# A fp32 convolution block with MLP on one core: seven output jobs as a 512- and a 256-column product a tile, with another evacuation

## The chip, the cores and the metric

The kernel runs on one core of one Trainium2 chip. The metric is the device time of one execution in microseconds (us). Three executions of the kernel before took 1066.16, 1066.22 and 1066.40 us; the median is 1066.22 us.

## The reference

```python
cond = jax.nn.silu(c)
mod = cond @ mod_w + mod_b
sh1, sc1, g1, sh2, sc2, g2 = jnp.split(mod, 6, axis=-1)
h = _rms_norm(x, norm1_g) * (1.0 + sc1) + sh1
y = _conv_mixer(h, conv_w_in, conv_b_in, ...)     # ends with u @ w_out + b_out
x = x + (1.0 + g1) * y
h = _rms_norm(x, norm2_g) * (1.0 + sc2) + sh2
u = jnp.square(jax.nn.relu(h @ mlp_w1))
x = x + (1.0 + g2) * (u @ mlp_w2)
```

There are 256 tokens and 2048 features; the MLP is 8192 wide. All is fp32. The part in question is `u @ w_out + b_out`, the gate `1 + g1`, the residual sum, and what the second norm and its shift `sh2` need from them.

## The kernel before

**Products.** Each fp32 operand is split in two fp32r halves, hi (the rounded value) and lo (the rest). A product is hi·hi + hi·lo + lo·hi. For weights `split_w` makes hi on ScalarE (L236) and lo on VectorE or GpSimd (L240), in two instructions a tile, each for 8 of the 16 blocks k of 128 input features. For activations `split_act` makes hi (L251, ScalarE) and lo (L254, VectorE), and they lie side by side as 512 columns.

**The output stage.** It lies from about 298 to 381 us. Job ("out", i), i = 0 to 7, makes 256 of the 2048 output features in two tiles c = 0, 1 of 128 features by 256 tokens. GpSimd makes lo for jobs 1 to 5, VectorE for jobs 6 and 7. Job 0 has a loop of its own (`mm_pair`). Jobs 1 to 7 call `mm(..., merged=True)`: for each k three products of 256 columns (L264 to L266) into one 256-column sum, both tiles in one PSUM tile `acc` of 512 columns, of which there are two. `mm` without `merged` makes two products for each k: L268, hi weights by the 512 columns, and L269, lo weights by the first 256, into the second half of a sum of 512 columns.

**Behind each job.** ScalarE applies the gate and a bias for each tile (L1419, in place in PSUM), VectorE adds 512 columns of x (L1420), ScalarE squares (L1422), GpSimd adds the squares up (L1427), ScalarE scales x by `1 + sc2` (L1431, into a tile `two` in SBUF), and L251 and L254 split that into `xa[i]`, the input of the first MLP jobs.

**Condition columns.** Beside the output jobs the 16 columns of `sh2` are made, each from 1 MB of `mod_w`: loaded by SyncE's queue into a `raw` buffer and multiplied with the condition on VectorE. Where the condition lies in PSUM (copied by L1441) that takes two instructions (L665), elsewhere one with two SBUF operands of 2048 columns (L669). The sum of the shift is copied by L1453 into `shz`, and `shift_row` (L600) multiplies it with the weights of ("up", 0) into a PSUM tile `row`.

**Behind job 7.** TensorE does a column sum of the squares (L695, ones by `sqacc`), the first 14 k of tile 0 of job ("up", 0, 0) with `xa[0]` to `xa[6]`, the column sum of job 7's squares (L695), L600, and then the products with `xa[7]`, the k 14 and 15.

**What orders the work.** The kernel is built by a scheduler that places each instruction by its data and its place in the code; `urgent()` puts a piece ahead, `tc.issue_after(x)` puts it behind x, and `after[job]` lists the columns that are made beside a job. `state["next_hi"]` is the weight split behind which job 6's L1419 goes. The instructions of one engine run strictly in the order that results.

Of the kernel before, what the change touches and what calls it, by code (L numbers as in the profile page):

```python
# [9 lines left out]
F32 = mybir.dt.float32  # L10
F32R = mybir.dt.float32r
AF = mybir.ActivationFunctionType
ALU = mybir.AluOpType
PSUM = bass.MemoryType.PSUM

P = 128
T = 256
# [18 lines left out]
SH1, SC1, G1, SH2, SC2, G2 = range(6)  # L36
# [51 lines left out]
def conv_block(ctx: ExitStack, tc: tile.TileContext, x, vec, dwq, c_row, mod_r, mod_t, mod_c, w_first, w_in, w_out, w1, w2, out):  # L88
    nc = tc.nc
# [49 lines left out]
    state = {"used": 0}  # L139
# [12 lines left out]
    def urgent():  # L152
        return tc.high_priority(offset=URGENT)
# [95 lines left out]
    def split_act(dst, src, on_act=True):  # L249
        if on_act:  # L250
            state["hi_end"] = nc.scalar.activation(dst[:, :, 0:T], src, AF.Copy).ins  # L251
        else:
            nc.vector.tensor_copy(dst[:, :, 0:T], src)
        state["lo_end"] = nc.vector.tensor_tensor(dst[:, :, T : 2 * T], src, dst[:, :, 0:T].bitcast(F32), op=ALU.subtract).ins  # L254

    def mm(p, c, key, acts_of, ks=range(KT), merged=False):
        halves = parts[key]
        for k in ks:
            hi, lo = halves[k // HALF]
            m = acts_of[k // 2][:, k % 2, :]  # L260
            if merged:
                out_p, begin, end = p[:, c, 0:T], k == 0, k == KT - 1
                w = hi[:, k % HALF, :]
                nc.tensor.matmul(out_p, w, m[:, 0:T], start=begin, stop=False)  # L264
                nc.tensor.matmul(out_p, w, m[:, T : 2 * T], start=False, stop=False)  # L265
                state["mm_end"] = nc.tensor.matmul(out_p, lo[:, k % HALF, :], m[:, 0:T], start=False, stop=end)  # L266
                continue
            nc.tensor.matmul(p[:, c, :], hi[:, k % HALF, :], m, start=(k == 0), stop=(k == KT - 1))  # L268
            state["mm_end"] = nc.tensor.matmul(  # L269
                p[:, c, T : 2 * T], lo[:, k % HALF, :], m[:, 0:T], start=False, stop=(k == KT - 1),  # L270
                skip_group_check=True,
            )
# [25 lines left out]
    def mm_tokens(sums, job, acts_of, last):  # L298
        steps = [(k, r) for k in range(HALF) for r in sums]
        if last:  # L300
            steps = [(k, r) for r in sums for k in range(HALF)]
        for k, (t, cs, p) in steps:
            hi, lo = [w[:, 4 * (k % 2) : 4 * (k % 2) + 4, :].rearrange("p k n -> p (k n)")[:, cs]
                      for w in parts[job + (k // 4,)][k // 2 % 2]]
            at = HALF * (job[2] % 2) + k
            m = acts_of[at // 2][:, at % 2, :]
            shared = job[0] == "down" and job[1] in EIGHT
            begin, end = at == 0 or shared and job[2] == 1 and t == 1 and at == HALF, at == KT - 1
            p_hi, p_lo = [m[:, n : n + P] for n in (t * P, T + t * P)]
            nc.tensor.matmul(p, p_hi, hi, start=begin, stop=False, skip_group_check=shared)  # L310
            nc.tensor.matmul(p, p_hi, lo, start=False, stop=False, skip_group_check=shared)  # L311
            nc.tensor.matmul(p, p_lo, hi, start=False, stop=end, skip_group_check=shared)  # L312

    def run_tasks():
        state["job"] += 1
        with tc.issue_after(state["w_lo"]), tc.issue_after(state["w_hi"]):
            for task in tasks.pop(state["job"], []):
                task()
# [371 lines left out]
    def mcol(which, k):  # L690
        return modc[:, which * KT + k : which * KT + k + 1]
# [21 lines left out]
    def ps_two():  # L713
        return ps.tile([P, 2, T], F32, name="acc", bufs=2)

    def two():
        return tmp.tile([P, 2, T], F32, name="two", bufs=6)

    def pair_of(tiles, k2):
        if tiles is xs:  # L720
            return xs[:, 2 * k2 : 2 * k2 + 2, :]
        return tiles[k2 // 2][:, 2 * (k2 % 2) : 2 * (k2 % 2) + 2, :]
# [51 lines left out]
    after = {}  # L774
# [34 lines left out]
    def splits(job):  # L809
        if job[0] == "eight":  # L810
            with urgent():
                split_eight(*job[1:])
            return
        if job[0] == "seven":
            with urgent():
                split_seven(*job[1:])
            return
        for c in range(2):
            if job + (c,) in parts_early:
                continue  # L820
            on_pool = job[0] == "in" or job in POOLED
            with urgent(), behind(c):
                split_w(job + (c,), nc.gpsimd if on_pool else nc.vector)
            if c == 0:
                state["next_hi"] = state["w_hi"]
                if job[0] in ("up", "down"):
                    with urgent():
                        run_tasks()

    def evac(p, cs=slice(0, 2), out=None):  # L830
        t1 = two()[:, cs, :]
# [347 lines left out]
    for n, job in enumerate(jobs):  # L1179
# [49 lines left out]
                    top_up()  # L1229
            continue  # L1230
        if kind == "out" and i > 0:
            p = ps_two()
        elif not by_tokens(job):
            p = ps.tile([P, 2, 2 * T], F32, name="mm", bufs=2)
        if by_tokens(job) and (i % 2 == 0 or kind == "down" and job[1] in EIGHT and i < 4):
# [2 lines left out]
        if job == ("up", 0, 0):  # L1238
            mm(p, 0, job + (0,), xa, range(SIDE))
            for at in range(2 * UNSCALED):  # L1240
                shift_row(at, shown.pop(("up", 0, at // 2, at % 2)))
            fold_shift()
            mm(p, 0, job + (0,), xa, range(SIDE, KT))
            mm(p, 1, job + (1,), xa)
        elif job == ("out", 0):
            for k2 in range(HALF):
                with tc.issue_after(state["row_end"].ins) if k2 == 1 else ExitStack():
                    mm_pair(p, job, k2)
                if k2 == 0:
                    with tc.issue_after(state["mm_end"].ins):  # L1250
                        mod_chunk(*last_row[0][1:], last_row[1])
        elif job in K_OUTER:
            for k2 in range(HALF):
                for c in range(2):
                    mm(p, c, job + (c,), xa if plain else hl, range(2 * k2, 2 * k2 + 2))
        elif kind == "in":
            rows = [key for key in after[job] if key[0] != "col"] if i < KT - 1 else []
            for c in range(2) if i < KT - 1 else (1, 0):
                for ks in (range(HALF), range(HALF, KT)):
                    with tc.issue_after(state.pop("rows_end")) if "rows_end" in state else ExitStack():  # L1260
                        mm(p, c, job + (c,), hl, ks, i == KT - 1)
            if not CONV_AT.get(n):
                with tc.issue_after(state["mm_end"].ins):
                    mods(rows)
                state["rows_end"] = state["row_end"].ins
        elif by_tokens(job):
            mm_tokens(sums[kind, i // 2], job, u2 if kind == "down" else hl, n == len(jobs) - 1)
        else:
            for c in range(2):
                mm(p, c, job + (c,), hl, merged=kind == "out")  # L1270
        with tc.issue_after(state["mm_end"].ins) if kind == "in" else ExitStack():
            mod_finish()
        if n == KT - 3:
# [136 lines left out]
        if kind == "out":  # L1410
            if i == 0:
                xs = take(("x", 0))
            t2 = p[:, :, 0:T]
            xp = pair_of(xs, i)
            with urgent():
                for c in range(2):
                    k = 2 * i + c
                    with tc.issue_after(state["next_hi"]) if i == HALF - 2 else ExitStack():
                        nc.scalar.activation(t2[:, c, :], t2[:, c, :], AF.Identity, scale=mcol(G1, k), bias=gb[:, k : k + 1])  # L1419
                nc.vector.tensor_tensor(xp, t2, xp, op=ALU.add)  # L1420
            ss = two()
            nc.scalar.activation(ss, xp, AF.Square)  # L1422
            if i == 0:
                nc.gpsimd.tensor_tensor(sqacc, ss[:, 0, :], ss[:, 1, :], op=ALU.add)
            elif i < HALF - 1:
                for c in range(2):
                    nc.gpsimd.tensor_tensor(sqacc, sqacc, ss[:, c, :], op=ALU.add)  # L1427
            a = two()
            for c in range(2):
                k = 2 * i + c  # L1430
                nc.scalar.activation(  # L1431
                    a[:, c, :], pair_of(xs, i)[:, c, :], AF.Copy, scale=amps[SC2][:, k : k + 1]
                )
            xa[i] = mp.tile([P, 2, 2 * T], F32R, name="u2", bufs=HALF)
            split_act(xa[i], a)
            if i == IN_PSUM[0]:
                state["cond"] = []
                for h in range(2):
# [3 lines left out]
                    state["cond"].append(half)  # L1442
            if i == IN_PSUM[-1] + 1:
                del state["cond"]
            mods(after[job])
            if i == HALF - 2:
                table(AF.Abs_reciprocal_sqrt, ss[:, 0, 0:1])
            if i == HALF - 1:
# [147 lines left out]
```

## Time and profile before

| | |
|---|---|
| median of three executions | 1066.22 us |
| profiled execution | 1066.46 us |
| its span | 1064.7 us |
| TensorE busy | 1046.3 us (98%) |
| VectorE busy | 911.7 us (86%) |
| ScalarE busy | 601.5 us (56%) |
| GpSimd busy | 222.3 us (21%) |
| DMA, mean over the span | 311 GB/s |

The span is cut out of the profiled execution; 1.8 us lie around it. Busy time is the union of an engine's instructions. In a timeline "x4" is a run of four like instructions with the time of all; "[0.58 <-DVE u L254]" is idle time of the engine ahead of the row and what ended it. L numbers are lines of the kernel before, except where the text says of the change. Matmul records overlap: the pace is the distance from start to start. PE is TensorE, DVE VectorE, ACT ScalarE, POOL GpSimd, SP SyncE.

### The profile page before, as it was taken

The page shows a single profiled execution, that of the slowest core. Times are in us where ns is not written, and L with a number is a line of the kernel's source. Part 1 is how long each engine was busy: PE and PEld are TensorE (multiplying, and loading weights), DVE is VectorE, ACT ScalarE, POOL GpSimd, SP SyncE. Part 2 cuts the span into 40 slices and gives each one's busy share as a digit, 9 for nine tenths or more (in the row PEclk, how much of TensorE's full clock was granted, in tenths as well). Part 3 has the DMA queues.
Part 4 walks back from the last instruction along what each step waited for, and adds up shares of the span by engine and source line. Part 5 has one row for each costly group of instructions (what it writes and reads, how often), then busy time and mean ns, then how long its engine had stood idle before and what let it go on. Part 6 is the DMA issues. An engine that isn't in the chain of part 4 may idle for free.

```text
span 1064.7 us, 15463 instructions
## 1 busy us (share of the span) xinstructions
PE 1046.3 (98%) x5776; PEld 865.1 (81%) x5776; DVE 911.7 (86%) x1191; ACT 601.5 (56%) x831; POOL 222.3 (21%) x153
## 2 busy tenths in 40 slices
PE   6999999999999999999999999999999999999998
PEld 3888886678699988888888888888888888888886
DVE  5777789998766889878799899899999899899996
ACT  4111298866775585344546565745566744656751
POOL 0000078989689272000000000000000000000001
PEclk8999999999999999999999999999999999999999
DMA  9999997996999976999996998693989796899853
GB/s 381 421 420 420 415 419 315 356 396 237 404 399 406 409 259 261 322 312 327 320 327 248 340 277 271 240 388 108 366 244 321 249 335 179 290 282 347 216 148 59
DMA packets 154333, 330.99 MB, mean 311 GB/s; under 512 B 88465, under 2 KB 114321, under 8 KB 119313
## 3 DMA queue, kind: packets, MB, share of 16 engines
q1 hardware_dynamic: 153248, 328.30, 85.1%
q0 software_dynamic: 864, 1.57, 1.1%
q8 instruction: 45, 0.74, 0.3%
q14 instruction: 30, 0.25, 0.1%
q10 hardware_dynamic: 146, 0.13, 0.0%
HBM read 313.71 MB, written 17.83 MB: 311 GB/s over the span
## 4 chain that ended last, share of the span: by engine, by line
PE 83%; DMA 10%; DVE 5%; ACT 1%; issue 1%; SPq 0%; DVEq 0%; ACTq 0%
PE mm L311 12%; PE mm L312 12%; PE mm L310 12%; DMA raw<-mod_c 9%; PE mm L268 6%; PE mm L269 3%; PE acc L265 3%; PE acc L264 3%; PE acc L266 3%; PE mm L1094 2%; PE row L576 2%; PE acc L485 2%; PE acc L486 2%; PE acc L484 1%; DVE raw L669 1%; DVE lo L240 1%
## 5 line engine op out<-in xcount | busy, mean ns | idle before, releaser
L236 ACT ACTIVATE hi<-raw 128x1024 fp32r<-128x1024 f32 x374 | 383.9, 1055 | 257.7 <-PE mm L312 127.6
L240 DVE TENSOR_TENSOR lo<-raw,hi 128x1024 fp32r<-128x1024 f32 x313 | 371.0, 1217 | 52.4 <-ACT hi L236 51.8
L240 POOL TENSOR_TENSOR lo<-raw,hi 128x1024 fp32r<-128x1024 f32 x61 | 155.8, 2581 | 30.1 <-ACT hi L236 29.8
L669 DVE SCALAR_TENSOR_TENSOR raw<-raw,cond 128x2048 f32<-128x2048 f32 x50 | 117.7, 2356 | 25.2 <-DMA raw<-mod_c 25.2
L460 POOL DMA_DIRECT2D out<-two x6 | 5.4, 902 | 639.2 <-DVE two L458 629.8
L311 PE MATMUL mm<-lo,u 128*128 128x512 f32 x320 | 124.5, 389 | 0.0
L312 PE MATMUL mm<-hi,u 128*128 128x512 f32 x320 | 124.0, 389 | 0.0
L310 PE MATMUL mm<-hi,u 128*128 128x512 f32 x320 | 123.8, 389 | 0.0
L310 PE MATMUL mm<-hi,hl 128*128 128x512 f32 x288 | 112.1, 389 | 0.0
L312 PE MATMUL mm<-hi,hl 128*128 128x512 f32 x288 | 112.1, 389 | 0.0
L311 PE MATMUL mm<-lo,hl 128*128 128x512 f32 x288 | 112.1, 389 | 0.0
L973 DVE SCALAR_TENSOR_TENSOR acc<-u,v,acc 128x256 f32<-128x256 f32 x230 | 91.5, 482 | 0.0
L268 PE MATMUL mm<-hl,hi 128*128 128x512 f32 x256 | 91.1, 399 | 0.0
L269 PE MATMUL mm<-hl,lo 128*128 128x256 f32 x256 | 71.7, 280 | 0.0
L310 PEld LDWEIGHTS mm<-hi,u 128*128 128x128 f32 x320 | 60.1, 188 | 12.6
L312 PEld LDWEIGHTS mm<-hi,u 128*128 128x128 f32 x320 | 60.1, 188 | 12.4
L311 PEld LDWEIGHTS mm<-lo,u 128*128 128x128 f32 x320 | 60.1, 188 | 12.4
L877 PE MATMUL mm<-two,first 128*128 128x256 f32 x240 | 56.7, 391 | 8.5 <-ACT two L935 8.5
L264 PE MATMUL acc<-hl,hi 128*128 128x256 f32 x224 | 63.4, 283 | 0.0
L265 PE MATMUL acc<-hl,hi 128*128 128x256 f32 x224 | 63.4, 283 | 0.0
L266 PE MATMUL acc<-hl,lo 128*128 128x256 f32 x224 | 63.4, 283 | 0.0
L310 PEld LDWEIGHTS mm<-hi,hl 128*128 128x128 f32 x288 | 54.1, 188 | 11.3
(383 smaller groups left out, 2018.8 us busy)
## 6 DMA issues: line engine op xcount, KB each, us to landing
raw<-w SPq DMA_DIRECT2D x128, 1024.0 KB, 7.6
raw<-mod_c SPq DMA_DIRECT2D x64, 1024.0 KB, 11.5
raw<-mod_r SPq DMA_DIRECT2D x28, 1024.0 KB, 8.7
raw<-w_in SPq DMA_DIRECT2D x16, 1024.0 KB, 10.6
raw<-w_out SPq DMA_DIRECT2D x16, 1024.0 KB, 8.2
first<-w_first SPq DMA_DIRECT2D x15, 1024.0 KB, 19.8
u<-kept SPq DMA_DIRECT2D x24, 512.0 KB, 7.6
flat<-two SPq DMA_DIRECT2D x30, 256.0 KB, 7.8
```

What stands on the lines that cost most here:

```text
L236: state["w_hi"] = nc.scalar.activation(hi, w[:, ks, :], AF.Copy).ins
L240: end = by.tensor_tensor(lo, w[:, ks, :], hi.bitcast(F32), op=ALU.subtract)
L264: nc.tensor.matmul(out_p, w, m[:, 0:T], start=begin, stop=False)
L265: nc.tensor.matmul(out_p, w, m[:, T : 2 * T], start=False, stop=False)
L266: state["mm_end"] = nc.tensor.matmul(out_p, lo[:, k % HALF, :], m[:, 0:T], start=False, stop=end)
L268: nc.tensor.matmul(p[:, c, :], hi[:, k % HALF, :], m, start=(k == 0), stop=(k == KT - 1))
L269: state["mm_end"] = nc.tensor.matmul(p[:, c, T : 2 * T], lo[:, k % HALF, :], m[:, 0:T], start=False, stop=(k == KT - 1), skip_group_check= ...
L310: nc.tensor.matmul(p, p_hi, hi, start=begin, stop=False, skip_group_check=shared)
L311: nc.tensor.matmul(p, p_hi, lo, start=False, stop=False, skip_group_check=shared)
L312: nc.tensor.matmul(p, p_lo, hi, start=False, stop=end, skip_group_check=shared)
L669: end = nc.vector.scalar_tensor_tensor(w, w, 1.0, cb, op0=ALU.mult, op1=ALU.mult, accum_out=acc)
L973: end = nc.vector.scalar_tensor_tensor(out, s, w, acc, op0=ALU.mult, op1=ALU.add)
```

## The change

Jobs 1 to 7 no longer merge: each k is L268 and L269, into a 512-column sum of its own for each tile, so that the two `acc` buffers hold one tile each. The bias is added to x in advance on ScalarE (`add_bias`, L1421 of the change). A tile is evacuated by two VectorE instructions of 256 columns (L1445 of the change), x += gate · half; the second waits for the first. ScalarE's L1419 and VectorE's L1420 remain for job 0 alone. The scaled x goes to PSUM, into the tiles `small` and `row` in turn (L1463 of the change), and L251 and L254 read it there; job 7 has `row`. The columns of `after[job]` are split between the two tiles and put behind the evacuation of each. The copies of the condition (L1431 of the change) stand ahead of the evacuation, and `next_hi` is gone.

```diff
--- before.py
+++ after.py
@@ -821,11 +821,9 @@
             on_pool = job[0] == "in" or job in POOLED
             with urgent(), behind(c):
                 split_w(job + (c,), nc.gpsimd if on_pool else nc.vector)
-            if c == 0:
-                state["next_hi"] = state["w_hi"]
-                if job[0] in ("up", "down"):
-                    with urgent():
-                        run_tasks()
+            if c == 0 and job[0] in ("up", "down"):
+                with urgent():
+                    run_tasks()
 
     def evac(p, cs=slice(0, 2), out=None):
         t1 = two()[:, cs, :]
@@ -1229,7 +1227,7 @@
                     top_up()
             continue
         if kind == "out" and i > 0:
-            p = ps_two()
+            p = [ps_two().rearrange("p a t -> p (a t)")[:, None, :] for _ in range(2)]
         elif not by_tokens(job):
             p = ps.tile([P, 2, 2 * T], F32, name="mm", bufs=2)
         if by_tokens(job) and (i % 2 == 0 or kind == "down" and job[1] in EIGHT and i < 4):
@@ -1265,9 +1263,12 @@
                 state["rows_end"] = state["row_end"].ins
         elif by_tokens(job):
             mm_tokens(sums[kind, i // 2], job, u2 if kind == "down" else hl, n == len(jobs) - 1)
+        elif kind == "out":
+            for c in range(2):
+                mm(p[c], 0, job + (c,), hl)
         else:
             for c in range(2):
-                mm(p, c, job + (c,), hl, merged=kind == "out")
+                mm(p, c, job + (c,), hl)
         with tc.issue_after(state["mm_end"].ins) if kind == "in" else ExitStack():
             mod_finish()
         if n == KT - 3:
@@ -1410,29 +1411,18 @@
         if kind == "out":
             if i == 0:
                 xs = take(("x", 0))
-            t2 = p[:, :, 0:T]
             xp = pair_of(xs, i)
-            with urgent():
+
+            def add_bias(k2, after):
                 for c in range(2):
-                    k = 2 * i + c
-                    with tc.issue_after(state["next_hi"]) if i == HALF - 2 else ExitStack():
-                        nc.scalar.activation(t2[:, c, :], t2[:, c, :], AF.Identity, scale=mcol(G1, k), bias=gb[:, k : k + 1])
-                nc.vector.tensor_tensor(xp, t2, xp, op=ALU.add)
-            ss = two()
-            nc.scalar.activation(ss, xp, AF.Square)
+                    k = 2 * k2 + c
+                    s = pair_of(xs, k2)[:, c, :]
+                    with urgent(), tc.issue_after(after):
+                        nc.scalar.activation(s, s, AF.Identity, bias=gb[:, k : k + 1])
+
             if i == 0:
-                nc.gpsimd.tensor_tensor(sqacc, ss[:, 0, :], ss[:, 1, :], op=ALU.add)
-            elif i < HALF - 1:
-                for c in range(2):
-                    nc.gpsimd.tensor_tensor(sqacc, sqacc, ss[:, c, :], op=ALU.add)
-            a = two()
-            for c in range(2):
-                k = 2 * i + c
-                nc.scalar.activation(
-                    a[:, c, :], pair_of(xs, i)[:, c, :], AF.Copy, scale=amps[SC2][:, k : k + 1]
-                )
-            xa[i] = mp.tile([P, 2, 2 * T], F32R, name="u2", bufs=HALF)
-            split_act(xa[i], a)
+                for k2 in (1, 2):
+                    add_bias(k2, state["silu"])
             if i == IN_PSUM[0]:
                 state["cond"] = []
                 for h in range(2):
@@ -1442,7 +1432,40 @@
                     state["cond"].append(half)
             if i == IN_PSUM[-1] + 1:
                 del state["cond"]
-            mods(after[job])
+            cols = list(after[job])
+            with urgent():
+                if i == 0:
+                    t2 = p[:, :, 0:T]
+                    for c in range(2):
+                        nc.scalar.activation(t2[:, c, :], t2[:, c, :], AF.Identity, scale=mcol(G1, c), bias=gb[:, c : c + 1])
+                    nc.vector.tensor_tensor(xp, t2, xp, op=ALU.add)
+            for c in range(2) if i else ():
+                with urgent():
+                    for a in range(2):
+                        end = nc.vector.scalar_tensor_tensor(
+                            xp[:, c, :], p[c][:, 0, T * a : T * a + T], mcol(G1, 2 * i + c), xp[:, c, :],
+                            op0=ALU.mult, op1=ALU.add,
+                        )
+                with tc.issue_after(end.ins):
+                    n_now = len(cols) // 2 if c == 0 and i < HALF - 1 else len(cols)
+                    mods(cols[:n_now])
+                    del cols[:n_now]
+            ss = two()
+            nc.scalar.activation(ss, xp, AF.Square)
+            if i == 0:
+                nc.gpsimd.tensor_tensor(sqacc, ss[:, 0, :], ss[:, 1, :], op=ALU.add)
+            elif i < HALF - 1:
+                for c in range(2):
+                    nc.gpsimd.tensor_tensor(sqacc, sqacc, ss[:, c, :], op=ALU.add)
+            a = ps.tile([P, 2, T], F32, name=("small", "row")[i % 2], bufs=1)
+            for c in range(2):
+                k = 2 * i + c
+                end = nc.scalar.activation(a[:, c, :], xp[:, c, :], AF.Copy, scale=amps[SC2][:, k : k + 1])
+            if 0 < i < HALF - 2:
+                add_bias(i + 2, end.ins)
+            xa[i] = mp.tile([P, 2, 2 * T], F32R, name="u2", bufs=HALF)
+            split_act(xa[i], a)
+            mods(cols)
             if i == HALF - 2:
                 table(AF.Abs_reciprocal_sqrt, ss[:, 0, 0:1])
             if i == HALF - 1:
```

Three places show how instructions move. The first is VectorE around the end of job 6. Before, the four L240 are the lo halves of job 7's weights, tile 0 and then tile 1:

```order
L1451 TENSOR_TENSOR rest_2502<-rest_2502,v 128x16 [waits DVE_49]
L240 TENSOR_TENSOR lo<-raw,hi 128x1024 [waits DMAHW6_49,PE_49,Activation_49]
L240 TENSOR_TENSOR lo<-raw,hi 128x1024 [waits PE_49,Activation_49]
L1420 TENSOR_TENSOR x_2504<-acc,x_2504 128x512 [waits Activation_49]
L240 TENSOR_TENSOR lo<-raw,hi 128x1024 [waits DMAHW7_49,PE_49,Activation_49]
L240 TENSOR_TENSOR lo<-raw,hi 128x1024 [waits PE_49,Activation_49]
```

In the change L1445 are the halves of tile 1 of job 6, and the four L240 the same lo halves:

```order
L1445 SCALAR_TENSOR_TENSOR x_2504<-acc,modc,x_2504 128x256 [waits PE_49]
L240 TENSOR_TENSOR lo<-raw,hi 128x1024 [waits DMAHW6_49,Activation_49]
L1445 SCALAR_TENSOR_TENSOR x_2504<-acc,modc,x_2504 128x256 [waits DVE_49]
L240 TENSOR_TENSOR lo<-raw,hi 128x1024 [waits Activation_49]
L240 TENSOR_TENSOR lo<-raw,hi 128x1024 [waits DMAHW7_49,Activation_49]
L240 TENSOR_TENSOR lo<-raw,hi 128x1024 [waits Activation_49]
```

The lo halves of tile 0 stood ahead of the residual sum of job 6; now the first stands behind the first half of the evacuation of job 6's last tile, and the second behind the other half.

The second place is VectorE around the end of job 7. Before, the L240 are the lo halves of the two tiles of job ("up", 0, 0), and L669 is a column of the shift:

```order
L240 TENSOR_TENSOR lo<-raw,hi 128x1024 [waits DMAHW1_49,PE_49,Activation_49]
L240 TENSOR_TENSOR lo<-raw,hi 128x1024 [waits PE_49,Activation_49]
L240 TENSOR_TENSOR lo<-raw,hi 128x1024 [waits DVE_49,DMAHW2_49,PE_49,Activation_49]
L240 TENSOR_TENSOR lo<-raw,hi 128x1024 [waits DVE_49,PE_49,Activation_49]
L669 SCALAR_TENSOR_TENSOR raw,modc<-raw,cond 128x2048 [waits DMAHW3_49]
L1420 TENSOR_TENSOR x_2504<-acc,x_2504 128x512 [waits Activation_49]
L1461 COPY gb<-v 128x16
L1452 TENSOR_TENSOR modc<-modc,rest_2502 128x16 [waits DVE_49]
L254 TENSOR_TENSOR u_3773<-two,u_3773 128x2x256 [waits Activation_49]
```

In the change the L1445 are the halves of tile 0 and of tile 1 of job 7 (the first half of tile 0 is one row further up), the L240 are the second lo half of tile 0 of ("up", 0, 0) and the two of its tile 1:

```order
L1445 SCALAR_TENSOR_TENSOR x_2504<-acc,modc,x_2504 128x256 [waits DVE_49]
L240 TENSOR_TENSOR lo<-raw,hi 128x1024 [waits Activation_49]
L240 TENSOR_TENSOR lo<-raw,hi 128x1024 [waits DMAHW2_49,Activation_49]
L1445 SCALAR_TENSOR_TENSOR x_2504<-acc,modc,x_2504 128x256 [waits PE_49]
L240 TENSOR_TENSOR lo<-raw,hi 128x1024 [waits Activation_49]
L669 SCALAR_TENSOR_TENSOR raw,modc<-raw,cond 128x2048 [waits DMAHW3_49]
L1445 SCALAR_TENSOR_TENSOR x_2504<-acc,modc,x_2504 128x256 [waits DVE_49]
L1475 TENSOR_TENSOR modc<-modc,rest_2502 128x16 [waits DVE_49]
L254 TENSOR_TENSOR u_3580<-row,u_3580 128x2x256 [waits Activation_49]
```

The last lo half and the column L669 now stand between the two halves of job 7's last tile, and two lo halves between the evacuations of tile 0 and tile 1.

The third place is ScalarE there. In the change, the first four L236 are the hi halves of tile 1 of ("up", 0, 0) and of tile 0 of ("up", 0, 1), whose lo halves GpSimd makes; L1463 into `row` is the scaled x of job 7, tile 0 first:

```order
L1463 ACTIVATE row<-x_2504,amp_122 128x256 [waits DVE_49]
L236 ACTIVATE hi<-raw 128x1024 [waits DMAHW2_49,PE_49]
L236 ACTIVATE hi<-raw 128x1024 [waits PE_49]
L236 ACTIVATE hi<-raw 128x1024 [waits DMAHW4_49,PE_49]
L236 ACTIVATE hi<-raw 128x1024 [waits PE_49]
L1454 ACTIVATE two<-x_2504 128x512 [waits DVE_49]
L1463 ACTIVATE row<-x_2504,amp_122 128x256 [waits Activation_49]
L1476 ACTIVATE shz<-modc 128x16 [waits DVE_49]
L236 ACTIVATE hi<-raw 128x1024 [waits DMAHW5_49,PE_49]
L251 ACTIVATE u_3580<-row 128x2x256 [waits Activation_49]
```

Before, the same stretch has the evacuation of job 7 (L1419) between the hi halves of those two tiles:

```order
L236 ACTIVATE hi<-raw 128x1024 [waits DMAHW2_49,PE_49]
L236 ACTIVATE hi<-raw 128x1024 [waits PE_49]
L1419 ACTIVATE acc<-acc,gb,modc 128x256 [waits PE_49]
L1419 ACTIVATE acc<-acc,gb,modc 128x256 [waits Activation_49]
L236 ACTIVATE hi<-raw 128x1024 [waits DMAHW4_49,DVE_49]
L236 ACTIVATE hi<-raw 128x1024 [waits DVE_49]
L1422 ACTIVATE two<-x_2504 128x512 [waits DVE_49,Pool_49]
L1431 ACTIVATE two<-x_2504,amp_122 128x256 x2
L1453 ACTIVATE shz<-modc 128x16 [waits DVE_49]
L236 ACTIVATE hi<-raw 128x1024 [waits DMAHW5_49,PE_49]
L251 ACTIVATE u_3773<-two 128x2x256 [waits Activation_49]
```

All four hi halves now stand behind the scaled x of job 7's tile 0, and ahead of the square of its whole x; two of them stood ahead of the evacuation. TensorE's order there is kept (L695, products, L695, L600, products), except that L600 waits for VectorE where it waited for ScalarE: `row` is free only when L254 of `xa[7]` has read it.

## Rows read from the trace of the kernel before

**Rows 1.** Windows: stretch, length, busy us (instructions) per engine, PEclk, DMA share, GB/s
```profile
298.00:381.00 83.00, 83.00 (x695) 83.00 (x694) 64.00 (x87) 53.14 (x77) 58.49 (x31) 1.00 0.97 389
381.00:397.00 16.00, 15.27 (x140) 13.03 (x140) 13.97 (x24) 12.30 (x24) 13.42 (x5) 1.00 0.64 235
```

**Rows 2.** Waits of TensorE in 298 to 397 us: in total, times, longest
```profile
PE mm L268 <- DVE u L254: 0.6, 1, 0.6
PE row L600 <- ACT shz L1453: 0.2, 1, 0.2
```

**Rows 3.** Timeline, start and length in us: merged products, the last ACT evacuations but one
```profile
297.96 0.28 PE L264 MATMUL acc<-hl,hi 128*128 128x256 f32 x1
298.32 0.28 PE L264 MATMUL acc<-hl,hi 128*128 128x256 f32 x1
...
369.61 1.11 ACT L1419 ACTIVATE acc<-acc,gb,modc 128x256 f32<-128x256 f32 x2 [5.67 <-PE acc L266]
```

**Rows 4.** Timeline of TensorE: pairs with loads running, pairs with few
```profile
188.20 0.40 PE L268 MATMUL mm<-hl,hi 128*128 128x512 f32 x1
...
191.03 0.40 PE L268 MATMUL mm<-hl,hi 128*128 128x512 f32 x1
...
381.70 0.40 PE L268 MATMUL mm<-u,hi 128*128 128x512 f32 x1
...
385.86 0.40 PE L268 MATMUL mm<-u,hi 128*128 128x512 f32 x1
```

**Rows 5.** Timeline of VectorE: the end of the output stage, one L254 from PSUM
```profile
300.38 0.69 DVE L254 TENSOR_TENSOR hl<-acc,hl 128x512 fp32r<-128x512 f32 x1 [3.73 <-ACT hl L251]
...
365.27 2.36 DVE L240 TENSOR_TENSOR lo<-raw,hi 128x1024 fp32r<-128x1024 f32 x2
...
382.45 2.28 DVE L669 SCALAR_TENSOR_TENSOR raw<-raw,cond 128x2048 f32<-128x2048 f32 x1
...
384.66 0.68 DVE L1420 TENSOR_TENSOR x<-acc,x 128x512 f32<-128x512 f32 x1
385.26 1.75 DVE L1461 COPY gb<-v 128x16 f32<-128x16 f32 x1
...
390.33 0.43 DVE L707 SCALAR_TENSOR_TENSOR small<-small,two 128x256 f32<-128x256 f32 x1
```

**Rows 6.** Timeline of GpSimd, and one VectorE instruction beside it
```profile
317.82 7.61 POOL L240 TENSOR_TENSOR lo<-raw,hi 128x1024 fp32r<-128x1024 f32 x3
...
320.79 2.38 DVE L254 TENSOR_TENSOR u<-two,u 128x512 fp32r<-128x512 f32 x1 [0.64 <-ACT u L251]
...
383.29 11.21 POOL L240 TENSOR_TENSOR lo<-raw,hi 128x1024 fp32r<-128x1024 f32 x4 [5.86 <-ACT hi L236]
```

**Rows 7.** Timeline of ScalarE behind the last evacuation
```profile
385.43 0.63 ACT L1422 ACTIVATE two<-x 128x512 f32<-128x512 f32 x1 [1.27 <-DVE x L1420]
...
387.12 0.23 ACT L1453 ACTIVATE shz<-modc 128x16 f32<-128x16 f32 x1 [0.26 <-DVE modc L1452]
387.24 1.04 ACT L236 ACTIVATE hi<-raw 128x1024 fp32r<-128x1024 f32 x1
388.19 0.62 ACT L251 ACTIVATE u<-two 128x512 fp32r<-128x512 f32 x1
```

**Rows 8.** Timeline of TensorE behind job 7
```profile
386.22 1.03 PE L695 MATMUL small<-two,ones 128*128 128x256 f32 x4
387.40 1.95 PE L600 MATMUL row<-raw,shz 128*32 128x128 f32 x64 [0.15 <-ACT shz L1453]
389.94 0.50 PE L268 MATMUL mm<-u,hi 128*128 128x512 f32 x1 [0.58 <-DVE u L254]
```

**Rows 9.** Start of the program: a wait of TensorE, and the clock behind it
```profile
20.14 4.02 PE L877 MATMUL mm<-two,first 128*128 128x256 f32 x9 [4.87 <-ACT two L935]
...
20.00:22.00 2.00, 1.86 (x4) 1.51 (x5) 1.96 (x4) 0.51 (x2) 0.00 (x0) 0.50 1.01 422
24.00:26.00 2.00, 2.00 (x11) 1.76 (x10) 0.62 (x3) 1.01 (x2) 0.00 (x0) 1.00 1.01 418
```

## The prediction

> **What bounds the kernel now.** The profile is read here from the engines' shares down to single rows. The windows show TensorE busy for all of 83.00 us of the output stage, and for 15.27 of the 16 us behind it [rows 1]. The list of TensorE's waits has two entries in that stretch, 0.6 and 0.2 us long [rows 2]. So TensorE bounds: what shortens its work there shortens the kernel, and any delay of it goes to the end unless later waits absorb it; there is less than 1 us of such waits. The timelines then give the paces, and where other engines stand ahead of the one place at which TensorE waits, the start of the MLP.
>
> **The products.** Three merged products start every 0.12 us, 0.36 us a k [rows 3]. A pair of 512 and 256 columns starts every 2.83 / 8 = 0.354 us with loads at full rate, and every 4.16 / 12 = 0.347 us when few run [rows 4]. Loads take 0.97 of the DMA engines in the stage [rows 1], so I take 0.3535: 0.0065 us for each of 224 pairs, **-1.45 us**; by the other pace it is -3.0. The Trainium skill (TensorE: Matmul & The Clock Gate, "Wait — 56ns, not 53.3ns?") gives N / 2.4 GHz + 2.5 ns for a product of N columns. By that the pair would save one 2.5 ns overhead, 0.56 us in all, as an estimate; no row supports so little, since both forms run slower than that here.
>
> **The evacuation in the stage.** VectorE has no L1445 before. Its nearest rows are L707, 256 columns with one PSUM operand, 0.43 us, and L1420, twice the columns, 0.68 us [rows 5]. So one costs 0.43 to 0.68; I take 0.45, since L707 has its size. The 28 take 12.6 us (19 at most), and 6 L1420 go, 4.1 us. VectorE is busy 64.0 of 83 us [rows 1], so it has room for these 8.5 us (15 at most). ScalarE loses 12 L1419 and gains 14 like ones that add the bias: zero, in 30 us of idle time. L254 reading PSUM takes 0.69 us [rows 5]; reading SBUF beside GpSimd it took 2.38 [rows 6], so this part gives time back. An `acc` buffer must be free one tile, 5.66 us, after its tile ends, and two halves take about 1 us: covered, unless VectorE is 4 us behind. The condition copies and biases only come sooner. Columns behind the evacuations free their `raw` buffers up to some 5 us later, and SyncE's loads queue behind those; what covers it is weights loaded ahead, and the DMA share of 0.64 after the stage [rows 1]. If the cover fails, each us of lateness is a us of TensorE. I count nothing.
>
> **The start of job 7.** This is certain from the order. Let E be the end of job 6. Before, it is 0.2 us ahead of ScalarE's evacuation at 369.61 [rows 3], 369.41; after 12 tiles at the new pace it is 369.41 - 12 x 0.104 = 368.16. The lo half for tile 0 of job 7 was made at 365.27 [rows 5]. Now it stands behind the first evacuation half of job 6's last tile: E + 0.2 for the signal + 0.45 + 1.18 (half of 2.36) = E + 1.85. TensorE wants it at E + 0.2 for its first 256-column product: **+1.65 us**, idle.
>
> **The end of job 7.** All times are from E. Tile 0 of job 7 ends at 1.65 + 5.66 = 7.3, tile 1 at 12.95. VectorE, from 1.85: a half 0.45, three lo halves 3.6, L669 2.28 [rows 5], L254 0.7, giving 8.9; the first half of tile 0 to 9.3, a lo half to 10.5, the second half to 10.95. ScalarE waits for that with its scaled x (0.45), and only then makes the hi halves, 1.0 each: at 12.45 and 13.45 those of tile 1 of ("up", 0, 0), at 14.45 and 15.45 those that GpSimd needs. VectorE's next lo half ends at 13.65, so the first half of tile 1, ready at 13.15, ends at 14.1, and the last lo half at 15.3.
>
> Now GpSimd comes in. Three rows show that a VectorE instruction with two SBUF operands and a GpSimd instruction exclude each other for their whole length. L254 at 320.79 ends at 323.2, just past the second of GpSimd's three, which takes a third of 7.61 us and so ended by 322.9 [rows 6]. L669 runs until 384.73, 1.44 us past 383.29, where GpSimd's four begin; they take 11.21 us, and without those 1.44 it is 2.44 each [rows 5, 6]. The copy behind it, a trifle, takes 1.75 us, until GpSimd's first is over [rows 5]. In the changed order GpSimd asks at 14.45, inside VectorE's lo half, and I take it that it gets its turn when that ends, as in the last two of these rows: 15.3 to 17.7. L669 follows until 20.0, the second half of job 7's last tile (one PSUM operand) until 20.45. GpSimd's second runs from 20.0 to 22.4, and the sum of the shift (two SBUF operands) waits for it: 22.6. Then ScalarE: `shz` 0.23, a hi half 1.04, L251 0.62 [rows 7], in all 24.5. VectorE's L254 frees `row` at 25.2. Only then L600 starts, and it takes 1.95 [rows 8]: TensorE goes on with `xa[7]` at E + 27.2 = 395.35. Before it did so at 389.94 [rows 8]. That is **+5.4 us**, and it holds the two terms above, -1.45 and +1.65; the rest, 5.2, is the late end. TensorE idles twice, for about 3 us each: it has its 14 pairs done at 12.95 + 0.25 + 14 x 0.3535 = 18.15, gets the square at 21.1, is done with L695 (1.03) [rows 8] at 22.2, and waits until 25.2.
>
> **Behind it** the MLP starts 5.4 us later, as do the modulations; their weights are loaded by then, and I find no wait that shrinks in exchange: TensorE has none there but those of 0.6 and 0.2 us, which this sum has used already [rows 2]. The sum is 1066.46 + 5.4 = 1071.9 for the profiled execution, 0.24 us above the median, so 1071.6 by the median. A measurement can tell about 0.2%, 2.1 us, from no change.
>
> **The rivals.**
> 1. **No collision.** If GpSimd gets its turn earlier, or never between VectorE's instructions, L669 runs from 15.3 to 17.6, the second half ends at 18.05, `shz` at 18.5, and L600 starts at 20.8 instead of 25.2: 4.4 less, +1.0, **1067.2**, no slowdown that can be measured. For it: GpSimd's start hangs on ScalarE's hi halves to within 1 us. Against it: the rows show that the loser waits a whole instruction of 2.4 us, and GpSimd has two of them. With one turn out of two it is +3.2, **1069.5**.
> 2. **The gain alone, not slower.** If the two lo halves and the tail are ready in time, only the faster products are left: -1.45 (-3.0 at the other pace), **1064.8** (1063.2). It decides at one point: lo of job 7 before E + 0.2. The order of VectorE speaks against it, since that instruction cannot pass one that waits for job 6's end.
> 3. **The clock falls.** TensorE waited 4.87 us at 20 us, and the granted clock in 20 to 22 us was 0.50, back at 1.00 in 24 to 26 [rows 9]. Up to 4 us of work at half the rate would add up to 2 us to mine: **1073.6**. The two waits of 3 us are shorter and have work between them; no row shows such a wait. The Trainium skill (TensorE: Matmul & The Clock Gate, Part 1) has the idle array fall to 1.2 GHz, which agrees with the 0.50 of these rows.
> 4. **Loads late.** Columns that free buffers later hold SyncE's queue, and TensorE waits for weights in or behind the stage: 2 us or more, 1074 and above. Against it stands the spare DMA time behind the stage [rows 1].
>
> **How the numbers follow.** Forecast (1070.3 to 1072.8) 0.42; no collision 0.19; one turn of two 0.16; clock 0.12; loads late 0.06; gain alone 0.05. The range of 1066.6 to 1074.4 takes in the first four and the unknown price of L1445, 0.45 or 0.68, which on the chain to L254 is about 1 us; it leaves out the last two and the tails. Faster by over 0.2% needs more than the gain alone at the likely pace: 0.04. Within 0.2%: no collision and most of the gain alone, 0.23. Slower: 0.73.
>
> **What would show it.** Right: L268 and L269 in the stage 0.354 us apart; TensorE waiting about 1.65 us at the start of job 7 for VectorE's lo; a GpSimd L240 between VectorE's last lo half and L669, and another ahead of the sum of the shift; L600 waiting for L254, at about E + 25; the following `xa[7]` product at about 395. Wrong: no wait of TensorE at job 7, L669 at 2.3 us straight behind the lo half, or TensorE waiting for loads or evacuations in jobs 1 to 6.

## The result, and the profile after

The changed kernel takes 1073.68 us (median of six runs, 1073.09 to 1074.89), the kernel before 1066.26 (six runs). The ratio is 1.0068, 95% interval 1.0058 to 1.0078: 7.4 us slower. 1071.6 was forecast, in a range of 1066.6 to 1074.4.

The profiled execution took 1073.09 us, 6.6 more than the profiled one of before. The list of TensorE's waits from 290 to 420 us, where before had 0.6 and 0.2 us [rows 2]:

```profile
PE small L695 <- ACT two L1454: 2.8, 1, 2.8
PE row L600 <- DVE u L254: 2.1, 1, 2.1
PE acc L269 <- DVE lo L240: 1.5, 1, 1.5
```

All three were forecast, as 3, 3 and 1.65 us. The timeline of TensorE shows them in their places (start, length, idle time ahead):

```profile
297.84 0.40 PE L268 MATMUL acc<-hl,hi 128*128 128x512 f32 x1
...
369.88 0.39 PE L269 MATMUL acc<-hl,lo 128*128 128x256 f32 x1 [1.47 <-DVE lo L240]
...
381.05 0.59 PE L695 MATMUL small<-sqacc,ones 128*128 128x256 f32 x2
...
389.26 1.69 PE L695 MATMUL small<-two,ones 128*128 128x256 f32 x4 [2.76 <-ACT two L1454]
393.08 3.61 PE L600 MATMUL row<-raw,shz 128*32 128x128 f32 x64 [2.13 <-DVE u L254]
396.61 0.50 PE L268 MATMUL mm<-u,hi 128*128 128x512 f32 x1
```

The last row is the product with `xa[7]`, at 389.94 before [rows 8]: 6.7 us later, which is the 6.6 us of the whole. Before it, L695 took 1.03 and L600 1.95 us [rows 8]; now they take 1.69 and 3.61. The windows of the same stretch say why (columns as in [rows 1], the granted clock behind the busy times):

```profile
388.00:390.00 2.00, 0.74 (x3) 0.63 (x4) 2.00 (x4) 1.00 (x2) 2.00 (x1) 0.92 0.43 66
390.00:392.00 2.00, 0.95 (x3) 0.23 (x1) 0.38 (x1) 1.47 (x3) 0.46 (x2) 0.50 0.93 393
392.00:394.00 2.00, 0.92 (x20) 0.84 (x24) 1.43 (x3) 1.50 (x4) 2.00 (x1) 0.50 1.07 446
394.00:396.00 2.00, 2.00 (x44) 1.81 (x40) 1.89 (x5) 0.79 (x2) 0.25 (x1) 0.50 0.35 147
396.00:398.00 2.00, 2.00 (x24) 1.45 (x17) 1.97 (x6) 1.16 (x4) 0.00 (x0) 0.87 0.96 279
```

From 390 to 396 us the clock stands at 1.2 GHz instead of 2.4. Around the wait of 1.47 us it stays at 1.00:

```profile
368.00:370.00 2.00, 0.53 (x4) 0.21 (x3) 1.79 (x3) 1.65 (x2) 0.00 (x0) 1.00 1.04 434
```

The timelines of VectorE and GpSimd show the late lo half, behind L1445, and the late end that leads to the first two waits of that list (L1484 is the copy that was L1461 before):

```profile
366.07 0.16 DVE L1484 COPY gb<-v 128x16 f32<-128x16 f32 x1
...
368.21 0.48 DVE L1445 SCALAR_TENSOR_TENSOR x<-acc,modc,x 128x256 f32<-128x256 f32 x1 [0.91 <-PE acc L269]
368.61 1.21 DVE L240 TENSOR_TENSOR lo<-raw,hi 128x1024 fp32r<-128x1024 f32 x1
369.75 0.48 DVE L1445 SCALAR_TENSOR_TENSOR x<-acc,modc,x 128x256 f32<-128x256 f32 x1
...
382.51 1.22 DVE L240 TENSOR_TENSOR lo<-raw,hi 128x1024 fp32r<-128x1024 f32 x1
383.64 4.50 DVE L669 SCALAR_TENSOR_TENSOR raw<-raw,cond 128x2048 f32<-128x2048 f32 x1
...
388.07 0.47 DVE L1445 SCALAR_TENSOR_TENSOR x<-acc,modc,x 128x256 f32<-128x256 f32 x1
388.47 1.91 DVE L1475 TENSOR_TENSOR modc<-modc,rest 128x16 f32<-128x16 f32 x1
392.33 0.69 DVE L254 TENSOR_TENSOR u<-row,u 128x512 fp32r<-128x512 f32 x1 [1.95 <-ACT u L251]
```
```profile
382.91 7.44 POOL L240 TENSOR_TENSOR lo<-raw,hi 128x1024 fp32r<-128x1024 f32 x2 [9.28 <-ACT hi L236]
```

GpSimd asks at 382.91, inside VectorE's L240, and gets its turn when that ends, at about 383.7. L669, 2.28 us alone [rows 5], takes 4.50; it ends at 388.14, when GpSimd's second turn begins. That ends at 390.35, and the sum of the shift, 128 by 16, which takes 0.17 us where GpSimd is idle (the first experiment), ends at 390.38 after 1.91. The Trainium skill (SBUF — State Buffer, "SBUF: two separate sides") calls the shared pair of ports an exclusive lock that the one who starts first holds for the whole instruction. The rows agree; they also show the two engines taking turns, instruction by instruction.

### The profile page after: what moved, and what is told of

Same layout as the page of the kernel before. It is cut to its first block, busy times and chain, and to the rows that moved or that the text cites. A ratio compares the mean times of both kernels' runs of the same rounds, so it can differ in the third digit from the quotient of the medians.

```text
span 1071.3 us, 15032 instructions
## 1 busy us (share of the span) xinstructions
PE 1047.6 (98%) x5552; PEld 854.5 (80%) x5552; DVE 916.2 (86%) x1212; ACT 597.3 (56%) x831; POOL 218.3 (20%) x153
## 4 chain that ended last, share of the span: by engine, by line
PE 84%; DMA 8%; DVE 6%; ACT 1%; issue 1%; SPq 0%; DVEq 0%; ACTq 0%
PE mm L312 13%; PE mm L310 13%; PE mm L311 13%; DMA raw<-mod_c 7%; PE mm L268 6%; PE acc L268 4%; PE mm L269 3%; PE acc L269 2%; PE mm L1092 2%; DVE raw L669 2%; PE row L576 2%; PE acc L485 2%; PE acc L486 2%; DVE lo L240 1%; PE acc L484 1%
## 5 line engine op out<-in xcount | busy, mean ns | idle before, releaser
L236 ACT ACTIVATE hi<-raw 128x1024 fp32r<-128x1024 f32 x374 | 381.6, 1053 | 219.0 <-PE mm L312 90.4
L240 DVE TENSOR_TENSOR lo<-raw,hi 128x1024 fp32r<-128x1024 f32 x313 | 371.4, 1219 | 36.2 <-ACT hi L236 35.6
L240 POOL TENSOR_TENSOR lo<-raw,hi 128x1024 fp32r<-128x1024 f32 x61 | 154.7, 2562 | 41.3 <-ACT hi L236 40.9
L669 DVE SCALAR_TENSOR_TENSOR raw<-raw,cond 128x2048 f32<-128x2048 f32 x50 | 116.5, 2332 | 34.2 <-DMA raw<-mod_c 34.2
L268 PE MATMUL mm<-hl,hi 128*128 128x512 f32 x256 | 91.2, 400 | 0.0
L268 PE MATMUL acc<-hl,hi 128*128 128x512 f32 x224 | 79.2, 399 | 0.0
L269 PE MATMUL mm<-hl,lo 128*128 128x256 f32 x256 | 71.9, 281 | 0.0
L269 PE MATMUL acc<-hl,lo 128*128 128x256 f32 x224 | 62.9, 281 | 1.5 <-DVE lo L240 1.5
L311 PEld LDWEIGHTS mm<-lo,hl 128*128 128x128 f32 x288 | 54.1, 188 | 11.2
```

Of the source, the lines that this page charges most:

```text
L236: state["w_hi"] = nc.scalar.activation(hi, w[:, ks, :], AF.Copy).ins
L240: end = by.tensor_tensor(lo, w[:, ks, :], hi.bitcast(F32), op=ALU.subtract)
L269: state["mm_end"] = nc.tensor.matmul(p[:, c, T : 2 * T], lo[:, k % HALF, :], m[:, 0:T], start=False, stop=(k == KT - 1), skip_group_check= ...
L669: end = nc.vector.scalar_tensor_tensor(w, w, 1.0, cb, op0=ALU.mult, op1=ALU.mult, accum_out=acc)
```

## The experiments

The theory is the prediction's, with the clock added to it: a late lo half (1.5 us), a late end through VectorE's order and GpSimd's turns (some 5 us), and a clock that falls behind the waits (some 2 us), against pairs that give 1.4 us. Its rivals are in the expectations. The kernels ran in two groups, each beside runs of the kernel before: those with GpSimd later, nine products, the lo halves ahead (first occasion) and the products undone beside a median of 1066.31 us, the others beside 1066.42.

**GpSimd asks later.**

```diff
+    state["gate"] = nc.gpsimd.tensor_copy(warm[:, 1:2], modc[:, SH2 * KT : SH2 * KT + 1]).ins
...
+    with tc.issue_after(state["gate"]) if key == ("up", 0, 1, 0) else ExitStack():
         end = by.tensor_tensor(lo, w[:, ks, :], hi.bitcast(F32), op=ALU.subtract)
```

> The change with one instruction more: GpSimd copies one column of the finished shift, and its lo halves for tile 0 of (up, 0, 1) are ordered behind that. VectorE's and ScalarE's orders stay. If GpSimd's turns on the shared port make the late end (my theory): L669 at 383.6 takes 2.3 us instead of 4.5, the sum of the shift 0.2 instead of 1.9, L600 starts about 389 instead of 393.1, no wait of TensorE is longer than 2 us, the clock stays at 1.00, and the time is 1067.5 to 1068.5. If the port only shifts waits and the order of VectorE alone makes the late end (rival): under 1 us less, 1072.7 to 1074.

1069.61 us (five runs, 1068.37 to 1070.75), ratio 1.0031 (1.0018 to 1.0044): 4.1 us under the change. The timeline of VectorE and TensorE in its profile (lines are one lower than in the change):

```profile
383.74 2.29 DVE L670 SCALAR_TENSOR_TENSOR raw<-raw,cond 128x2048 f32<-128x2048 f32 x1
...
386.35 0.17 DVE L1476 TENSOR_TENSOR modc<-modc,rest 128x16 f32<-128x16 f32 x1
...
389.81 1.96 PE L601 MATMUL row<-raw,shz 128*32 128x128 f32 x64 [1.53 <-DVE u L255]
...
542.43 0.50 PE L312 MATMUL mm<-lo,u 128*128 128x512 f32 x1 [1.56 <-DVE lo L241]
```
```profile
388.00:390.00 2.00, 0.47 (x10) 0.20 (x12) 0.82 (x2) 1.94 (x5) 2.00 (x2) 1.00 0.98 410
```

L669 and the sum have their own lengths again, 2.2 and 1.7 us less, though VectorE's order is the same: GpSimd's turns did that. L600 starts 3.3 us sooner, the two waits fall to 0.7 and 1.5 us, and the clock stays at 1.00 from 384 to 400. The profiled run, the slowest of the five, has a wait of 1.6 us at 542 and one of 0.6 us elsewhere in the MLP, which no trace of before or of the change shows. The median is above the 1067.5 to 1068.5 that was expected, the fastest run lies in it; that the runs between have such a later wait too was not seen, and why it comes is open.

**TensorE kept busy.** Nine products with results that nobody reads stand ahead of job 7's column sum; the second kernel has the four behind it as well, the first has not.

```diff
+    if i == HALF - 1:
+        spare = ps_two()
+        for m in range(9):
+            nc.tensor.matmul(spare[:, 0, :], ones, xp[:, 0, :], start=True, stop=True)
...
     column_sum(sp[:, 0:T], [sqacc, ss[:, 0, :], ss[:, 1, :]])
+    for m in range(4):
+        nc.tensor.matmul(spare[:, 0, :], ones, ss[:, 1, :], start=True, stop=True)
```

> The change with nine products more on TensorE (ones by x of job 7's tile 0, 256 columns fp32, into a sum that nobody reads), placed among the 14 pairs ahead of the column sum, some 4.5 us of work: nothing that TensorE waits for becomes ready sooner, but it waits only some 0.5 us. If the halved clock after the two waits costs time of its own: L600 takes 1.95 us instead of 3.6, the granted clock stays at 1.00 from 390 to 398, and the time falls by 1.5 to 2.5 us, to 1071.2 to 1072.2, with less scatter between runs. If the clock costs nothing beside the waits (rival): 1073.5 or more, since nothing else is sooner.

> As e5_busy (nine idle products ahead of the column sum of job 7), and four more between that sum and L600, about 1.9 us, in the wait of 2.0 us that e5_busy kept. VectorE's order is that of the change; nothing that TensorE waits for is sooner. If the waits lower the clock and the clock costs time (theory): granted clock 1.00 through 390 to 398, L600 takes 1.95 us (3.61 in the change, 3.07 in e5_busy), and 1070.3 to 1071.3, 1 us under e5_busy or more. If a lower clock is not due to idle time (rival): L600 over 3 us again and about 1072.1 or more.

With nine: 1072.11 us (four runs, 1071.25 to 1072.97), ratio 1.0052 (1.0035 to 1.0069). With thirteen: 1071.68 us (four runs, 1071.44 to 1071.78), ratio 1.0047 (1.0031 to 1.0062). L600 and one window of the clock, of the first:

```profile
392.96 3.07 PE L600 MATMUL row<-raw,shz 128*32 128x128 f32 x64 [1.96 <-DVE u L254]
```
```profile
394.00:396.00 2.00, 2.00 (x41) 1.62 (x33) 1.87 (x5) 0.00 (x0) 0.14 (x1) 0.50 0.67 188
```

and of the second:

```profile
392.99 1.95 PE L600 MATMUL row<-raw,shz 128*32 128x128 f32 x64 [0.23 <-DVE u L254]
```
```profile
394.87 0.50 PE L268 MATMUL mm<-u,hi 128*128 128x512 f32 x1
```
```profile
394.00:396.00 2.00, 2.00 (x42) 1.67 (x34) 1.89 (x6) 0.89 (x3) 0.18 (x1) 1.00 0.88 229
```

L600 starts at the same time in both and in the change (393.08) to within 0.1 us, so nothing else got sooner. The product with `xa[7]` starts at 394.87 instead of 396.61, 1.7 us sooner, by L600's length alone. Work without use made the kernel 2.0 us faster than the change by the medians, 1073.68 to 1071.68, and 1.3 by the profiled executions, 1073.09 to 1071.78: the clock's price lies in 1.3 to 2.0 us. The intervals of the two ratios overlap, but every run of the thirteen lies under every run of the change.

With nine products one wait of 1.96 us is left, and the clock still falls behind it, which was expected wrongly, as was less scatter (the four runs spread over 1.7 us); the time agreed with the expectation all the same, since the clock was low for less long. The thirteen were expected at 1070.3 to 1071.3 and 1 us under the nine; the clock is as expected, the time 0.4 above, and 0.4 under the nine.

**The lo halves of job 7 ahead.**

```diff
+    if c == 0 and job == ("out", HALF - 1):
+        state["next_hi"], state["next_lo"] = state["w_hi"], state["w_lo"]
...
-    with urgent():
+    with urgent(), tc.issue_after(state["next_lo"]) if i == HALF - 2 and c else ExitStack():
         for a in range(2):
             end = nc.vector.scalar_tensor_tensor(
...
-    end = nc.scalar.activation(a[:, c, :], xp[:, c, :], AF.Copy, ...)
+    with tc.issue_after(state["next_hi"]) if i == HALF - 2 else ExitStack():
+        end = nc.scalar.activation(a[:, c, :], xp[:, c, :], AF.Copy, ...)
```

> The change with the evacuation of job 6's last tile ordered behind the two lo halves of job 7's tile 0 (and ScalarE's scaled x of job 6 behind their hi halves). With it the scheduler also puts job 7's two halves closer together and L600 behind the products with the last input pair. If order on VectorE is the whole loss (theory): no wait of TensorE at the start of job 7, waits under 1 us in all behind it, and 1064.8 to 1066.3, the gain of the pairs left over. If the evacuation tile by tile on VectorE itself costs more than the pairs give (rival): waits of TensorE for evacuations or splits somewhere else in the stage, and 1068 or more.

> The kernel of e1_lo_first once more, to see on another occasion whether it beats the kernel before. If its gain is the pairs (1.35 us by the stage's length) and the vanished waits (0.7): 1064.4 to 1065.0, with its interval below 1. If it was chance: within 0.3 us of before.

1064.67 us (ten runs, 1064.45 to 1065.19), 0.1 under what was expected, ratio 0.9985 (0.9976 to 0.9994); on the other occasion 1064.74 us (eleven runs, 1064.53 to 1066.93), the same ratio and interval. It beats both kernels, before by 1.6 us. TensorE has no wait from 290 to 430 us in either profile. VectorE and TensorE in the first:

```profile
367.25 2.36 DVE L240 TENSOR_TENSOR lo<-raw,hi 128x1024 fp32r<-128x1024 f32 x2
369.52 1.00 DVE L1447 SCALAR_TENSOR_TENSOR x<-acc,modc,x 128x256 f32<-128x256 f32 x2
...
385.62 1.75 DVE L1478 TENSOR_TENSOR modc<-modc,rest 128x16 f32<-128x16 f32 x1
```
```profile
297.88 0.40 PE L268 MATMUL acc<-hl,hi 128*128 128x512 f32 x1
...
379.50 0.59 PE L695 MATMUL small<-sqacc,ones 128*128 128x256 f32 x2
...
390.19 1.96 PE L600 MATMUL row<-raw,shz 128*32 128x128 f32 x64
```

The sum of the shift is held by GpSimd here too (1.75 us), and it costs nothing: L600 stands behind the products with `xa[7]`, which TensorE does meanwhile. But this edit changed the order at both ends, so it does not say which end cost what.

**The late end alone.**

```diff
-    a = ps.tile([P, 2, T], F32, name=("small", "row")[i % 2], bufs=1)
+    a = two() if i == HALF - 1 else ps.tile([P, 2, T], F32, name=("small", "row")[i % 2], bufs=1)
```

> The change, but the scaled x of job 7 alone goes to a tile in SBUF as before, so that L600 need not wait for the L254 that reads row. VectorE's order at the end of job 6 stays that of the change (first lo half behind the first evacuation half); at the end of job 7 the scheduler puts the second half ahead of L669, GpSimd's hi halves behind job 7's split, and L600 behind the products with the last input pair. If the loss is the sum of a late lo (1.5 us) and the late end (theory): the wait of 1.5 us at the start of job 7 stays, no other wait over 0.5 us, clock 1.00, and 1066.0 to 1066.8, e1_lo_first plus 1.5. If the late lo caused the late end too (rival, since e1_lo_first removed both): TensorE waits 2 us or more behind job 7 and 1069 or more.

1066.02 us (ten runs, 1065.68 to 1068.42), ratio 0.9997 (0.9988 to 1.0006). The timelines of its profile:

```profile
369.96 0.39 PE L269 MATMUL acc<-hl,lo 128*128 128x256 f32 x1 [1.48 <-DVE lo L240]
```
```profile
369.82 0.48 DVE L1445 SCALAR_TENSOR_TENSOR x<-acc,modc,x 128x256 f32<-128x256 f32 x1
...
383.24 0.47 DVE L1445 SCALAR_TENSOR_TENSOR x<-acc,modc,x 128x256 f32<-128x256 f32 x1
383.63 2.28 DVE L669 SCALAR_TENSOR_TENSOR raw<-raw,cond 128x2048 f32<-128x2048 f32 x1
...
386.48 0.17 DVE L1475 TENSOR_TENSOR modc<-modc,rest 128x16 f32<-128x16 f32 x1
```
```profile
386.86 14.19 POOL L240 TENSOR_TENSOR lo<-raw,hi 128x1024 fp32r<-128x1024 f32 x6 [13.16 <-ACT hi L236]
```

TensorE's wait for the late lo is still there, the list of its waits has nothing else behind it, and the granted clock is 1.00 throughout 380 to 400 us. One tile in another memory, with the order that the scheduler makes of it, takes back 7.7 us (1073.68 less 1066.02), the whole loss and a little more, and the late lo is worth 1.3 us (1066.02 less 1064.7). GpSimd starts only when the sum of the shift is done, so neither L669 nor the sum meets it. The two ends are independent, as the theory had it; which of the moved instructions freed the late end, this kernel does not say.

**The products undone.**

```diff
-    mm(p[c], 0, job + (c,), hl)
+    mm(p[c], 0, job + (c,), hl, merged=True)
...
-    for a in range(2):
+    for a in range(1):
```

> The change with its products undone: three of 256 columns a k again, into one half of each tile's sum, so that one L1445 a tile is enough (7 us less on VectorE). By the rows, 14 tiles at 0.36 us a k cost 1.45 us more on TensorE than pairs. The scheduler here puts the first lo half of job 7 ahead of job 6's evacuation and lets the shift be summed behind the last split. Theory: no wait at the start of job 7, the end of the stage about as before, 1066.3 to 1068. Rival, that the pairs themselves are worth nothing and the new evacuation and ordering are bad: over 1070.

1065.49 us (ten runs, 1065.34 to 1065.78), ratio 0.9992 (0.9983 to 1.0001): slightly under the 1066.3 to 1068 expected. TensorE in its profile:

```profile
297.76 0.28 PE L264 MATMUL acc<-hl,hi 128*128 128x256 f32 x1
...
380.73 0.59 PE L695 MATMUL small<-sqacc,ones 128*128 128x256 f32 x2
```

From the first product of job 1 to the column sum it takes 82.97 us, as before (297.96 [rows 3] to 380.93). With pairs and no wait, in the kernel with the lo halves ahead, it takes 81.62: the pairs are worth **1.35 us**. TensorE has no wait behind job 7 here, and the 0.8 us between this kernel and before are about the 0.6 and 0.2 us of [rows 2]. So the new evacuation costs TensorE nothing with one VectorE instruction a tile; with two, the kernel with the lo halves ahead shows the same.

## Why the prediction was right, and where it was short

The prediction held the mechanism, the place and the sign; the size was 2.1 us short. Its steps:

- **The products**: 1.45 us, measured 1.35. The Trainium skill's rule for the pace (TensorE: Matmul & The Clock Gate, "Wait — 56ns, not 53.3ns?") gave 0.56 as an estimate; the 1.35 us do not agree with that.
- **The evacuation in the stage**: nothing, and nothing was measured. One L1445 takes 0.47 to 0.48 us where 0.45 was taken, and jobs 1 to 6 have no wait of TensorE, for loads or for `acc`. The 6 L1420 and 12 L1419 that the forecast counts as gone are those up to 381 us; with job 7's they are 7 and 14, which leaves the sum as it is.
- **The start of job 7**: 1.65 us, a wait of 1.47 in the profile, 1.3 by the time of the runs.
- **The end of job 7**: with E at 368.16, L669 was to end at 388.2, the sum of the shift at 390.8, and L600 to start at 393.4. They came at 388.14, 390.38 and 393.08. That GpSimd gets its turn where VectorE's L240 ends was an assumption, and it held. One of the three rows behind it was misread: L1461 has one SBUF operand and writes SBUF, and still it took 1.75 us beside GpSimd [rows 5], against 0.16 where GpSimd is idle (L1484).
- **The step that failed** is the next: "Only then L600 starts, and it takes 1.95". It took 3.61, and L695 1.69 instead of 1.03, since the clock had fallen behind the first wait and stayed low through the second. L695's 0.66 us went into the wait behind it, 2.1 where 3 were forecast; L600's 1.66 reach the end and put the product with `xa[7]` at 396.61 instead of 395.35. This was rival 3, priced at up to 2 us and given 0.12; keeping TensorE busy shows 1.3 to 2.0, and the kernel in which it is busy takes 1071.68 us (profiled execution 1071.78), where 1071.6 (1071.9) was forecast. The reason given against it, that waits of 3 us are shorter than the 4.87 us at the start and have work between them, was no reason, since no row of before has a wait of that length.
- **The rest of the 2.1 us**: the forecast was 1.2 us short in the profiled execution. The median of the change lies 0.6 above its profiled execution, where the forecast put it 0.24 below; what makes the other runs longer was not seen.
- **Behind it**: "I find no wait that shrinks in exchange" held in the profile: nothing came back, and 6.7 us at 396.61 are 6.6 at the end.

Rival 1, no collision, did not come, and its price was too high: taking GpSimd's turns away gives 3.3 us at L600, and not the 4.4 forecast, mainly because its sum goes from the end of the shift straight to `shz`, and leaves out the square and the scaled x that ScalarE makes first (386.46 to 387.46 in that kernel). Rival 2 fell where it was said to be decided, at VectorE's order; its price was right: with the lo halves ahead and the end in time, 1064.7 was measured, where 1064.8 was given. Rival 4, late loads, did not show in the change.

Open: the six runs of the change spread over 1.8 us, the six of before over 0.3 (of the 41 others of before, single ones lie up to 1.5 us above the median). In the kernel with the late GpSimd a later wait shows in the slowest run; whether the same makes the slower runs of the change was not seen, since its profiled run is the fastest. The late end was also not split between VectorE's order and the wait for `row` by itself: putting `a` in SBUF moved both.

## What to carry to other kernels

A cheap gain on the bounding engine (1.35 us here) is worth only what the order on the other engines leaves of it: after a change, look where a split that the next job needs first now stands behind an instruction that waits for the last job's end. Where VectorE and GpSimd both work on SBUF, look at what meets: here an instruction of 0.17 us on the path took 1.91 because GpSimd had just started. Moving GpSimd's instruction, or giving the bounding engine something else to do first, took that cost away. A wait of TensorE can cost more than its length: here the work behind two waits of 2 to 3 us ran at half the clock, for 1.3 to 2.0 us more, while waits of 1.5 us left the clock at 1.00.

## What the runs showed that was not expected

The granted clock fell to 0.50 behind a single wait of 1.96 us, with TensorE busy for 20 us ahead of it (the kernel with nine products more), and stayed at 1.00 with waits of 1.47, 1.53 and 0.7 us. Thirteen products without use, some 6 us of work, made a kernel 1.3 us (profiled execution) to 2.0 us (median) faster.
